# Low halves of the plain feed-forward, projection and gate weights: negated by ScalarE and completed by an adding transfer, instead of subtracted on VectorE

## The chip, the cores and the metric

The kernel runs on one core of one Trainium2 chip. The metric is the time of one execution on the device in microseconds (us); smaller is better. Several runs are taken and their median is compared. The profile is one further execution, recorded by the hardware. The core's engines are called here by the names that the profile uses: PE (TensorE, the matmuls), PEld (its weight loads), DVE (VectorE), ACT (ScalarE), POOL (GpSimd) and SP (SyncE, which issues transfers). Each engine works through its own queue in order, and waits on semaphores for the others.

## The reference

The kernel computes the trunk of a small encoder on 512 tokens of width 1024, in two layers. What matters here, cut from the reference:

```python
for i in range(DEPTH):                       # 2 layers
    h = h + 0.5 * swiglu(rmsnorm(h, ffn1_norm[i]), ffn1_w_gu[i], ffn1_w_down[i])
    hn = rmsnorm(h, mix_norm[i])
    h = h + (ssd_mixer(hn, ...) if i % 2 == 0 else neighbourhood_attention(hn, ...))
    h = h + 0.5 * swiglu(rmsnorm(h, ffn2_norm[i]), ffn2_w_gu[i], ffn2_w_down[i])
    gate = jax.nn.sigmoid(rmsnorm(h, ple_norm[i]) @ ple_w_gate[i])
    h = h + gate * rmsnorm(p[i] @ ple_w_proj[i], ple_post_norm[i])
```

`swiglu(x, w_gu, w_down)` splits `x @ w_gu` into a gate and an up half of 2816 columns each, and returns `(silu(gate) * up) @ w_down`. All of it is in 32-bit floating point.

## The kernel before

**Products in high and low halves.** A matmul of PE takes its operands in the type float32r, which holds fewer bits than float32. So the kernel splits each operand a into a high half, hi = a rounded to float32r, and a low half, lo = a - hi, and adds three products: hi by hi, hi by lo and lo by hi. In `gemm` these are lines 268, 271 and 272: line 268 multiplies the high half of the weights (`wh`) by the high half of the activations, line 271 the high half of the weights by the low half of the activations, and line 272 the low half of the weights (`wl`) by the high half of the activations. `block` does the same in lines 483, 484 and 485. An activation tile holds 512 tokens, so a matmul of `gemm` has 128 x 512 results, one of `block` 128 x 256.

**Units of weights.** Weights come in units of 128 partitions x 1024 numbers (512 KB), fewer for the down projections. A unit of 1024 feeds 24 matmuls: eight pieces of 128 rows, three products each. The generator `plan` writes down the order of all units of the program, ahead of the code that uses them. Its entries have a letter: "u" is a unit that is loaded and split; "g" loads a group of four, "s" forms sums and differences of them, "o" splits one of the results.

**Four steps of a unit.** `load_unit` (line 201) loads it by a transfer on SP into a raw buffer `wr`, of which there are four, up to three loads ahead. `split_raw` makes the halves: line 218, a copy on ACT from `wr` into `wh` that rounds, and line 220, a subtraction on DVE of `wh` from `wr` into `wl`. `wh` and `wl` have three buffers each. `unit` hands a unit to the matmuls; before it does, it prepares units until three are ready. So a unit is split as soon as the unit three places before it has left its buffers, that is, while PE works on the two units in between. The framework that builds the program turns all this into one queue for each engine, with the waits that the data and the buffers need, and it may queue instructions in another order than the text.

**The stages.** Each layer has four parts.

- A feed-forward part (`ffn`, four in the program). It begins with a *plain* stage: twelve units of `w_gu` (gate and up columns of the first six column blocks, `PLAIN`), one full `gemm` each, in `gate_up`. In all but the first part the first two of them run side by side, so that the factor of the norm can be formed meanwhile. During the plain stage DVE and ACT also form sums and differences of the activations (`sums`, lines 437 to 468) that the rest of the part needs. The rest is a *block* stage: eight pairs of column blocks by seven smaller products each, with the down projections between them (line 546 adds their results to `h`).
- In the first layer the state-space mixer (`ssd`), in the second the attention (`attention`).
- A second feed-forward part. Before its last eight down projections come the two units of `w_proj` (`ple_proj`), which feed eight products with two pieces each.
- A gate part (`ple`): eight units of `w_gate`, one `gemm` each. The activations of its norm are split by line 289 (ACT) and line 290 (DVE), each as soon as the last down projection of those rows has been added to `h` by line 546; their squares are summed by lines 310 (ACT) and 314 (POOL).

In the first feed-forward part of the program the first four plain units are loaded and split in halves by code of their own at the end of `trunk` (lines 1242 to 1247), not by `split_raw`.

**POOL's work around the change** is line 314 (sums of squares) and line 419 (the product of gate and up half), besides work in the mixer. No transfer is issued on POOL. `SCRATCH` sets aside 1024 bytes per partition for transfers that POOL issues.

Of the kernel before, what the change touches and what calls it, by code (L numbers as in the profile page):

```python
# [10 lines left out]
AF = mybir.ActivationFunctionType  # L11
ALU = mybir.AluOpType
# [36 lines left out]
def ffn_order():  # L49

    for f in range(PLAIN):
        yield "plain", f
    for c in range(1, len(CHUNKS)):
        a, b = CHUNKS[c]
        blocks = [(p, i) for p in range(a // 2, b // 2) for i in range(7)]
        d = 0
        for n, (p, i) in enumerate(blocks):
            yield "block", p, i  # L60
            while d < KD and (d + 0.5) * len(blocks) <= KD * (n + 1):
                yield "down", c - 1, d
                d += 1
    yield "between",
    for d in range(KD):
        yield "down", len(CHUNKS) - 1, d
# [3 lines left out]
def trunk(ctx, tc, A, out):  # L70
    nc = tc.nc
    v, s, g, te, sy = nc.vector, nc.scalar, nc.gpsimd, nc.tensor, nc.sync
# [13 lines left out]
    def nm(t):  # L86
        uid[0] += 1
        return f"{t}{uid[0]}"
# [54 lines left out]
    def plan():  # L143

        for i in range(stop):
            l, w = divmod(i, 4)
            if w in (0, 2):
                gu, gw, dn = [A[f"w_{x}{1 + w // 2}"][l] for x in ("gu", "gw", "dn")]  # L150

                def ahead(p, i_):
                    if i_ == 0:
                        yield "g", [gw[p - PLAIN // 2, x, y] for x, y in ((1, 0), (0, 0), (1, 1), (0, 1))]
                    yield "s", (p, i_)

                for what, *a in ffn_order():
                    if what == "plain":
                        for x in range(2):
                            yield "u", gu[a[0], x]  # L160
                            n = 2 * a[0] + x - (2 * PLAIN - 3)
                            if n >= 0:
                                yield from ahead(PLAIN // 2, n)
                    elif what == "block":
                        yield "o", a
                        if a[1] >= 4 and a[0] < NF // 2 - 1:
                            yield from ahead(a[0] + 1, a[1] - 4)
                    elif what == "down":
                        b = CHUNKS[a[0]]
                        yield "u", dn[a[1], :, b[0] * P:b[1] * P]  # L170
                    elif w == 2:
                        for n in range(2):
                            yield "u", A["w_proj"][l, n]
            elif w == 3:
                for n in range(KD):
                    yield "u", A["w_gate"][l, n]
            elif l % 2 == 0:
                for n in range(65):
                    yield "u", A["w_in"][n]
                for x in range(2):  # L180
                    for d in range(KD):
                        yield "u", A["w_out"][d, :, x * 1024:(x + 1) * 1024]
            else:
                for n in range(24):
                    yield "u", A["w_qkv"][n]
                for d in range(KD):
                    yield "u", A["w_ao"][d]

    todo = list(plan())

    loads = [x for what, a in todo if what in "gu"
             for x in (zip(a, ("wr", "wr", "md", "md")) if what == "g" else [(a, "wr")])]
    todo = iter(todo)
    raws, ready, splits, group, blocks = [], [], [], [], {}
    waiting = {"wr": 0, "md": 0}

    def load_unit():
        src, tag = loads.pop(0)
        raw = wp.tile([P, 1024], F32, name=nm("wr"), tag="wr", bufs=4) if tag == "wr" else wide()
        n = src.shape[-1]  # L200
        sy.dma_start(out=raw[:, :n], in_=src)
        raws.append((raw, n, tag))
        waiting[tag] += 1

    def take():
        if not raws:
            load_unit()
        raw, n, tag = raws.pop(0)
        waiting[tag] -= 1
        return raw, n  # L210

    def top_up():
        while loads and waiting[loads[0][1]] < {"wr": 3, "md": 2}[loads[0][1]]:
            load_unit()

    def split_raw(raw, n):
        hi = wp.tile([P, 1024], F32R, name=nm("wh"), tag="wh", bufs=3)
        splits.append(s.copy(out=hi[:, :n], in_=raw[:, :n]))  # L218
        lo = wp.tile([P, 1024], F32R, name=nm("wl"), tag="wl", bufs=3)
        v.tensor_sub(out=lo[:, :n], in0=raw[:, :n], in1=hi[:, :n])  # L220
        ready.append((hi, lo))

    def wide():
        return md().rearrange("p a b -> p (a b)")

    def prep_next():
        item = next(todo, None)
        if item is None:
            return False
        what, a = item  # L230
        if what == "u":
            split_raw(*take())
        elif what == "g":
            group[:] = [take()[0] for _ in range(4)]
        elif what == "s":
            p, i = a
            a21, a11, a22, a12 = group
            if i == 0:
                blocks[p] = {0: a11, 2: a21, 3: wide(), 4: a12, 6: a22}
                v.tensor_add(out=blocks[p][3], in0=a21, in1=a22)  # L240
            elif i == 1:
                blocks[p][1] = blocks[p][5] = wide()
                v.tensor_sub(out=blocks[p][1], in0=blocks[p][3], in1=a11)
            else:
                v.tensor_sub(out=a21, in0=a11, in1=a21)
        else:
            p, i = a
            b = blocks[p]
            split_raw(b[i], 1024)
            if i == 1:  # L250
                v.tensor_sub(out=b[5], in0=b[4], in1=b[5])
        top_up()
        return True

    def unit():
        while len(ready) < 3 and prep_next():
            pass
        return ready.pop(0)
# [969 lines left out]
    n = Norm(C_G1)  # L1228
# [36 lines left out]
    def first(pts, pairs):  # L1265
        done_ = [0] * 4
        here, cut_ = 0, [0] * 4
        for o in order:
            if isinstance(o, int):
                here = o + 1  # L1270
            else:
                cut_[o[0]] += 1
            for u in range(4):
                while done_[u] < min(here, 4 * cut_[u]):
                    k = done_[u]
                    gemm(pts[u], begun[u][2:], pairs[k:k + 1], first=k == 0, last=k == KD - 1, off=k)
                    done_[u] += 1
        while len(ready) < 3:
            prep_next()

        with tc.issue_after(splits[-1].ins):
            for k in range(KD):
                n.count(k, True)

    for i in range(stop):
        l, w = divmod(i, 4)
# [11 lines left out]
        n = m  # L1298
# [99 lines left out]
```

## Time and profile before

| what | value |
|---|---|
| runs | 2351.93, 2351.70 and 2353.02 us; median 2351.93 us |
| the profiled execution | 2352.96 us |
| its span, first to last instruction | 2351.2 us |
| mean clock granted to PE | 0.997 of full |
| transfers on SP's queue | 263.57 MB, 34.8% of the transfer engines' time |
| read from memory / written | 253.40 MB / 10.26 MB |

How to read the lines of the profile that follow. Times are us from the start of the span unless marked ns. A row of the timeline is: start, duration, engine, source line, operation, what it writes `<-` what it reads (tiles by name: `ps` is a matmul's result, `md` and `sc` are activations, `hs` is `h`, `t` a temporary), the shape, the count, and in brackets how long its engine had been idle before it and which instruction ended that. A row that groups instructions by line has the count and the shortest, median and longest duration in ns, then the starts of the first and the last of them. A row of a stretch of the span has the busy time of each engine in it, the clock granted to PE, and the share of time in which the 16 transfer engines were busy. Rows of transfers give the size of one and the median time from its issue to its landing. A matmul's duration overlaps with that of the next: at full speed 128 x 512 matmuls start about 0.23 us apart although each is shown as 0.39 us long.

Where the parts lie in the span, by the rows of the trace: the first feed-forward part up to about 370 us, its plain stage up to about 75; the state-space mixer up to about 923; the second feed-forward part from there, with its plain stage up to about 990 and its projection units at 1250; the first gate part from 1285 to 1339; the third feed-forward part with its plain stage from there; the attention from about 1660; the last feed-forward part from about 1935, its projection units at 2262, and the last gate part from 2296 to the end.

### The profile page before, as it was taken

To read this page: it belongs to the slowest core of one execution; us is meant where nothing else is said; L and a number is where in the kernel's file an instruction comes from. 1 tells how busy PE (TensorE), PEld (TensorE's weight loads), DVE (VectorE), ACT (ScalarE), POOL (GpSimd) and SP (SyncE) were. 2 spreads that over 40 slices of the span, in tenths; PEclk is the share of its full clock that TensorE was granted. 3 is DMA by queue.
4 is the path that set the end of the run, shared out by engine and by line. 5 is a ranking of instruction groups with operands and counts; after the bars stand their busy time and mean duration, and the time that the engine had idled before them with its cause. 6 is when DMAs were issued, how large, how long until landed. Compare 5 with 4: busy or idle time off the path is not lost.

```text
span 2351.2 us, 35169 instructions
## 1 busy us (share of the span) xinstructions
PE 2327.4 (99%) x13810; PEld 2026.6 (86%) x13810; DVE 1805.7 (77%) x2565; ACT 1111.8 (47%) x1819; POOL 353.7 (15%) x309
## 2 busy tenths in 40 slices
PE   9999999999999999999999999999999999999998
PEld 8899998888888888899997889999877888999987
DVE  7878868877777747978877897887778757777767
ACT  5433445755655653433345443334437744334353
POOL 1000001444445551100003110000100011000020
PEclk9999999999999999999999999999999999999999
DMA  5233324544444543323322332332433233333222
GB/s 191 84 101 104 108 72 131 172 138 138 143 136 142 162 162 107 115 84 104 108 86 84 103 115 85 104 108 77 145 121 130 103 100 100 111 108 99 81 81 81
DMA packets 99238, 265.95 MB, mean 113 GB/s; under 512 B 12016, under 2 KB 12912, under 8 KB 99072
## 3 DMA queue, kind: packets, MB, share of 16 engines
q1 hardware_dynamic: 98784, 263.57, 34.8%
q8 instruction: 108, 1.77, 0.3%
q14 instruction: 58, 0.48, 0.1%
q10 hardware_dynamic: 288, 0.14, 0.0%
HBM read 253.40 MB, written 10.26 MB: 112 GB/s over the span
## 4 chain that ended last, share of the span: by engine, by line
PE 90%; DVE 5%; ACT 1%; issue 1%; POOL 1%; DMA 1%; SPq 0%; POOLq 0%; ACTq 0%; DVEq 0%
PE ps L268 19%; PE ps L271 19%; PE ps L272 19%; PE ps L485 9%; PE ps L484 9%; PE ps L483 9%; PE ps L866 1%; DVE wl L220 1%; PE ps L844 1%; PE ps L887 1%; PE ps L800 1%; PE ps L786 1%; PE ps L1172 1%; DVE md L290 1%; DVE md L287 1%
## 5 line engine op out<-in xcount | busy, mean ns | idle before, releaser
L268 PE MATMUL ps<-md,wh 128*128 128x512 f32 x2128 | 838.4, 395 | 2.7 <-ACT md L286 2.1
L272 PE MATMUL ps<-md,wl 128*128 128x512 f32 x2128 | 830.7, 391 | 4.7 <-DVE wl L220 4.7
L271 PE MATMUL ps<-md,wh 128*128 128x512 f32 x2128 | 831.3, 391 | 0.7 <-DVE md L290 0.5
L218 ACT CAST wh<-wr 128x1024 fp32r<-128x1024 f32 (+2 forms) x401 | 358.1, 894 | 521.4 <-PE ps L271 199.9
L220 DVE TENSOR_TENSOR wl<-wr,wh 128x1024 fp32r<-128x1024 f32 (+2 forms) x401 | 429.0, 1070 | 114.1 <-ACT wh L218 85.3
L272 PEld LDWEIGHTS ps<-md,wl 128*128 128x128 f32 x2128 | 400.1, 188 | 90.7 <-DVE wl L220 6.7
L268 PEld LDWEIGHTS ps<-md,wh 128*128 128x128 f32 x2128 | 400.5, 188 | 84.4 <-issue 3.5
L271 PEld LDWEIGHTS ps<-md,wh 128*128 128x128 f32 x2128 | 400.9, 188 | 81.1 <-issue 3.3
L314 POOL TENSOR_TENSOR sq<-sq,sq 128x512 f32<-128x512 f32 x71 | 101.1, 1424 | 1444.8 <-ACT sq L310 1444.0
L218 ACT CAST wh<-md 128x1024 fp32r<-128x1024 f32 x160 | 167.7, 1048 | 297.8 <-PE ps L484 263.0
L483 PE MATMUL ps<-sc,wh 128*128 128x256 f32 x896 | 253.8, 283 | 4.2 <-ACT wh L218 4.2
L485 PE MATMUL ps<-sc,wl 128*128 128x256 f32 x896 | 254.3, 284 | 0.8 <-DVE wl L220 0.8
L484 PE MATMUL ps<-md,wh 128*128 128x256 f32 x896 | 254.1, 284 | 0.0
L485 PE MATMUL ps<-md,wl 128*128 128x256 f32 x896 | 254.1, 284 | 0.0
L484 PE MATMUL ps<-sc,wh 128*128 128x256 f32 x896 | 254.1, 284 | 0.0
L483 PE MATMUL ps<-md,wh 128*128 128x256 f32 x896 | 253.9, 283 | 0.0
L489 DVE TENSOR_TENSOR t<-ps,t 128x512 f32<-128x512 f32 x224 | 151.7, 689 | 129.8 <-PE ps L485 127.9
L220 DVE TENSOR_TENSOR wl<-md,wh 128x1024 fp32r<-128x1024 f32 x160 | 196.5, 1228 | 26.8 <-ACT wh L218 26.7
L483 PEld LDWEIGHTS ps<-sc,wh 128*128 128x128 f32 x896 | 172.1, 192 | 8.4 <-ACT wh L218 4.6
L484 PEld LDWEIGHTS ps<-sc,wh 128*128 128x128 f32 x896 | 172.2, 192 | 3.7
L484 PEld LDWEIGHTS ps<-md,wh 128*128 128x128 f32 x896 | 172.4, 192 | 1.2
L483 PEld LDWEIGHTS ps<-md,wh 128*128 128x128 f32 x896 | 172.4, 192 | 1.2
(207 smaller groups left out, 2859.8 us busy)
## 6 DMA issues: line engine op xcount, KB each, us to landing
wr<-in_w_in_dram SPq DMA_DIRECT2D x65, 512.0 KB, 3.5
wr<-in_w_gw_dram SPq DMA_DIRECT2D x64, 512.0 KB, 4.1
md<-in_w_gw_dram SPq DMA_DIRECT2D x64, 512.0 KB, 5.0
wr<-in_w_dn_dram SPq DMA_DIRECT2D x128, 256.0 KB, 2.7
wr<-in_w_gu_dram SPq DMA_DIRECT2D x44, 512.0 KB, 3.5
hs<-crow SPq DMA_DIRECT2D x64, 256.0 KB, 3.9
wr<-in_w_dn_dram SPq DMA_DIRECT2D x32, 384.0 KB, 3.1
wr<-in_w_qkv_dram SPq DMA_DIRECT2D x24, 512.0 KB, 3.7
```

What stands on the lines that cost most here:

```text
L218: splits.append(s.copy(out=hi[:, :n], in_=raw[:, :n]))
L220: v.tensor_sub(out=lo[:, :n], in0=raw[:, :n], in1=hi[:, :n])
L268: m = te.matmul(out=pt, lhsT=hi[:, sl], rhs=part(xp, 0, cols), start=first and k == 0, stop=False)
L271: te.matmul(out=pt, lhsT=hi[:, sl], rhs=part(xp, 1, cols), start=False, stop=False)
L272: te.matmul(out=pt, lhsT=lo[:, sl], rhs=part(xp, 0, cols), start=False, stop=last and k == n - 1)
L287: v.tensor_sub(out=dst[:, 1, :], in0=src, in1=dst[:, 0, :])
L290: v.scalar_tensor_tensor(out=dst[:, 1, :], in0=src, scalar=gain, in1=dst[:, 0, :], op0=ALU.mult, op1=ALU.subtract)
L314: (v if fast else g).tensor_add(out=self.acc, in0=self.acc, in1=q)
L483: te.matmul(out=o, lhsT=hi[:, sl], rhs=xh, start=j == 0 and kk == 0, stop=False)
L484: te.matmul(out=o, lhsT=hi[:, sl], rhs=xl, start=False, stop=False)
L485: te.matmul(out=o, lhsT=lo[:, sl], rhs=xh, start=False, stop=j == 1 and kk == 3)
L489: v.tensor_add(out=k[to], in0=pt, in1=k[other])
```

## The change

Units of the plain stages, of `w_proj` and of `w_gate` get a letter of their own in `plan`, "a". For them the low half is made without DVE. ACT reads the raw buffer a second time and writes its negative into the low half's buffer; that buffer has the type float32r, so what stands there is -hi. Then POOL issues a transfer that reads the same 512 KB of weights from memory once more and adds them to what stands in the buffer: the result is the weight minus hi, rounded to float32r as before. All other units keep the subtraction. `take` now hands on the source of the unit as well, so that the second transfer knows it.

```diff
                     if what == "plain":
                         for x in range(2):
-                            yield "u", gu[a[0], x]
+                            yield "a", gu[a[0], x]
...
                         for n in range(2):
-                            yield "u", A["w_proj"][l, n]
+                            yield "a", A["w_proj"][l, n]
             elif w == 3:
                 for n in range(KD):
-                    yield "u", A["w_gate"][l, n]
+                    yield "a", A["w_gate"][l, n]
...
-    def split_raw(raw, n):
+    def split_raw(raw, n, src=None):
         hi = wp.tile([P, 1024], F32R, name=nm("wh"), tag="wh", bufs=3)
         splits.append(s.copy(out=hi[:, :n], in_=raw[:, :n]))
         lo = wp.tile([P, 1024], F32R, name=nm("wl"), tag="wl", bufs=3)
-        v.tensor_sub(out=lo[:, :n], in0=raw[:, :n], in1=hi[:, :n])
+        if src is None:
+            v.tensor_sub(out=lo[:, :n], in0=raw[:, :n], in1=hi[:, :n])
+        else:
+            s.activation(out=lo[:, :n], in_=raw[:, :n], func=AF.Copy, scale=-1.0)
+            g.dma_start(out=lo[:, :n], in_=src, accum_op=ALU.add)
         ready.append((hi, lo))
...
-        if what == "u":
+        if what == "a":
             split_raw(*take())
+        elif what == "u":
+            split_raw(*take()[:2])
```

The entries of `raws` and the result of `take` get the source as a further member, and the list `loads` counts the letter "a" like "u". The first four plain units of the program stay as they were.

More of the change, by code (lines that the diff above doesn't have):

```diff
@@ L189, in trunk @@
     todo = list(plan())
-    loads = [x for what, a in todo if what in "gu"
+    loads = [x for what, a in todo if what in "agu"
              for x in (zip(a, ("wr", "wr", "md", "md")) if what == "g" else [(a, "wr")])]
@@ L201, in load_unit @@
         sy.dma_start(out=raw[:, :n], in_=src)
-        raws.append((raw, n, tag))
+        raws.append((raw, n, tag, src))
         waiting[tag] += 1
@@ L207, in take @@
             load_unit()
-        raw, n, tag = raws.pop(0)
+        raw, n, tag, src = raws.pop(0)
         waiting[tag] -= 1
-        return raw, n
+        return raw, n, src
     def top_up():
```

## The prediction

> **What bounds the kernel now.** I read the page's busy times and its chain first, then stretches of the span, then the waits inside the two stretches where the matmul engine (PE) is not full.
>
> ```profile
> span 2351.2 us, 35169 instructions
> PE 2327.4 (99%) x13810; PEld 2026.6 (86%) x13810; DVE 1805.7 (77%) x2565; ACT 1111.8 (47%) x1819; POOL 353.7 (15%) x309
> ...
> PE 90%; DVE 5%; ACT 1%; issue 1%; POOL 1%; DMA 1%; SPq 0%; POOLq 0%; ACTq 0%; DVEq 0%
> ```
>
> PE is busy for 2327.4 of 2351.2 us. The 23.8 us that are left hold the start and the tail too, so taking work off VectorE (DVE) can win only a few us, in places where PE visibly waits. Anything that makes PE wait costs its whole length.
>
> ```profile
> core 0: us, PE busy (x) PEld busy (x) DVE busy (x) ACT busy (x) POOL busy (x), PEclk, DMA share, GB/s
> 60.00:80.00 20.00, 15.81 (x71) 12.49 (x69) 19.86 (x33) 9.84 (x16) 1.55 (x1) 0.99 0.28 92
> 80.00:100.00 20.00, 19.18 (x107) 17.52 (x108) 16.79 (x20) 6.36 (x9) 2.07 (x1) 0.84 0.32 93
> 960.00:980.00 20.00, 20.00 (x90) 16.58 (x89) 19.09 (x30) 9.45 (x15) 1.64 (x1) 1.00 0.31 96
> 1280.00:1300.00 20.00, 17.85 (x74) 13.86 (x73) 18.52 (x31) 8.85 (x12) 4.52 (x3) 0.91 0.34 111
> 2290.00:2310.00 20.00, 16.68 (x73) 12.60 (x73) 18.70 (x24) 8.86 (x12) 5.32 (x4) 1.00 0.41 132
> ```
>
> The first two rows are the end of the plain stage of the first feed-forward part: DVE is full (19.86 of 20), PE loses 4.19 us, and in the next 20 us the granted clock is 0.84. The third row is the same stage of the second feed-forward part: DVE is nearly as full (19.09), yet PE has no gap; there DVE relief wins nothing. The last two rows are the starts of the two gate stages, with 2.15 and 3.32 us of PE idle beside a busy DVE.
>
> **The change, part by part.** It touches these units:
>
> ```profile
> wr<-in_w_gu_dram SPq DMA_DIRECT2D x44, 512.0 KB, 3.5
> ...
> wr<-in_w_gate_dram SPq DMA_DIRECT2D x16, 512.0 KB, 3.5
> ...
> wr<-in_w_proj_dram SPq DMA_DIRECT2D x4, 512.0 KB, 3.9
> ```
>
> That is 44 + 16 + 4 = 64 units (the four half-loaded ones at the start are formed elsewhere and stay). Each loses one DVE subtraction and gains one ScalarE (ACT) instruction and one GpSimd (POOL) transfer of 512 KB, 33.6 MB in all.
>
> ```profile
> L220 DVE TENSOR_TENSOR wl<-wr,wh x4: 1212/1216/1222, 51.1 to 65.9; 128x1024 fp32r<-128x1024 f32 x4
> ```
> ```profile
> L218 ACT CAST wh<-wr x2: 1040/1046/1052, 2293.7 to 2294.7; 128x1024 fp32r<-128x1024 f32 x2
> ```
>
> A subtraction is 1.22 us, so DVE gets 78 us lighter. The negation on ACT has the size of the cast, 1.05 us (two casts start 1.0 apart), so ACT gets about 67 us heavier, from 1111.8: it has room. Neither total is on PE's path; what counts is when a low half is ready.
>
> Let X be the time from the end of the negation to the landing of the added transfer. No row shows a POOL transfer or an added one. The nearest rows:
>
> ```profile
> wr<-in_w_dn_dram SPq DMA_DIRECT2D x128, 256.0 KB, 2.7
> ```
> ```profile
> L201 SPq DMA_DIRECT2D wr<-in_w_gu_dram x44: 327/328/388, 12.5 to 1978.2; - x44
> ```
>
> A plain load of 256 KB lands in 2.7 us and one of 512 KB in 3.5, 0.8 more per 256 KB. The added transfer must also fetch the 512 KB it adds to. If that counts like bytes loaded, it lands as 1 MB would, 5.1 us (an extrapolation). For the issue I add 0.7, about twice SP's 0.33. So X = 5.8. The low end is 3.5 (reading back is free); the high end is 7.0 (two loads in series), or 8.3 with one DVE instruction of about 1.2 us blocking on top. I take the middle because the step from 256 to 512 KB says bytes cost something.
>
> [...] No run here shows a POOL transfer yet.
>
> Now the places, each as "cast start + 2.0 (cast and negation) + X, against PE's first use".
>
> First feed-forward part (gain). DVE's four subtractions of the row above fall in the stretch that ends in PE's wait:
>
> ```profile
> 78.32 0.62 ACT L467 CAST md<-t 128x512 fp32r<-128x512 f32 x1 [2.53 <-DVE t L464]
> 78.85 1.04 ACT L218 CAST wh<-md 128x1024 fp32r<-128x1024 f32 x1
> ```
> ```profile
> 75.36 0.40 PE L271 MATMUL ps<-md,wh 128*128 128x512 f32 x1
> 79.94 0.58 PE L483 MATMUL ps<-sc,wh 128*128 128x256 f32 x1 [4.19 <-ACT wh L218]
> ...
> 81.55 0.58 PE L485 MATMUL ps<-sc,wl 128*128 128x256 f32 x1 [0.82 <-DVE wl L220]
> ```
> ```profile
> 86.41 0.42 PE L272 MATMUL ps<-md,wl 128*128 128x512 f32 x1
> ```
>
> PE waits 4.19 us for ACT, whose cast stands behind L467, which waits for DVE's backlog. Four subtractions less, 4 x 1.2 = 4.8 us, bring that forward by about the whole wait. What is late next is the low half behind the 0.82 wait, still DVE's. From 79.94 to 86.41 PE needs 6.47 us for the 24 matmuls of one block, 256 columns each; at half the 0.227 us of a 512-column one (worked out below) it would be 2.7, so 3.8 are lost, the 0.82 among them, and about 2.9 to the clock. Of the two gate stages, both with a wait of some 2 us, one lost clock (0.91) and the other didn't (1.00), so a short wait need not cost clock, and I count two thirds of the 2.9. Gain 4.2 + 1.9, about 6.0; bounds 3 (half the backlog moves) and 8.0 (all of it).
>
> Gate stages, two (about nothing). The first gate unit of the second one:
>
> ```profile
> 2296.39 0.39 PE L268 MATMUL ps<-md,wh 128*128 128x512 f32 x1
> 2296.62 0.39 PE L271 MATMUL ps<-md,wh 128*128 128x512 f32 x1
> 2299.06 0.50 PE L272 MATMUL ps<-md,wl 128*128 128x512 f32 x1 [2.06 <-DVE wl L220]
> ```
> ```profile
> L220 DVE TENSOR_TENSOR wl<-wr,wh x3: 1209/1214/1700, 2297.8 to 2304.3; 128x1024 fp32r<-128x1024 f32 x3
> ```
> ```profile
> L268 PE MATMUL ps<-md,wh x1: 387/387/387, 2306.2 to 2306.2; 128*128 128x512 f32 x1
> ```
> ```profile
> L268 PE MATMUL ps<-md,wh x18: 389/389/389, 2284.8 to 2296.4; 128*128 128x512 f32 x18
> ```
>
> Full speed is 11.56 us for 17 groups of three (last row), 0.68 a group, 0.227 a matmul, 5.44 a unit of 24. The unit begins at 2296.39 and its last group, held back by DVE's chain for the next norm, at 2306.21, so it ends at 2306.9. Afterwards DVE's chain is 3.9 us shorter (three subtractions), but the low half lands at 2293.7 + 2.0 + 5.8 = 2301.5 instead of before 2299.06. With 22 matmuls of 0.227 to go the unit ends at 2306.6. So one wait takes the place of another: no change at X = 6, a loss of 1 us for each us beyond, a gain below, up to 3.5. I take 0 for both.
>
> Projection units, two (a small loss). Cast and first use of the low half:
>
> ```profile
> L218 ACT CAST wh<-wr x1: 1047/1047/1047, 1244.0 to 1244.0; 128x1024 fp32r<-128x1024 f32 x1
> ```
> ```profile
> L272 PE MATMUL ps<-md,wl x1: 395/395/395, 1252.3 to 1252.3; 128*128 128x512 f32 x1
> ```
>
> 1244.0 + 2.0 + 5.8 = 1251.8, half a us before 1252.3. But two negations, 2.1 us, now stand on ACT ahead of the casts that PE's first matmul there waits for, and ACT, idle about half of the time, takes up perhaps 1.5 of it. Loss 0.6 each, 1.2 together, bounds 0 and 4.2 (both in full).
>
> Third-from-first plain unit of the other three feed-forward parts (nothing, with little to spare):
>
> ```profile
> L218 ACT CAST wh<-wr x2: 1037/1044/1050, 932.7 to 933.6; 128x1024 fp32r<-128x1024 f32 x2
> ```
> ```profile
> L272 PE MATMUL ps<-md,wl x1: 393/393/393, 941.1 to 941.1; 128*128 128x512 f32 x1
> ```
>
> 932.7 + 2.0 + 5.8 = 940.5 against 941.1: hidden up to X = 6.4, then 1 us per us, three times.
>
> All other plain and gate units are cast two units of PE ahead, 10.9 us, against 2.0 + 5.8: hidden up to X of about 8, counting a us of queueing. On POOL the transfer waits for ACT's negation; behind it stand only the gated product and the sums of squares, and POOL is idle 85% of the time. The raw buffer is no longer read by DVE, so loads on SP can start earlier; they are not waited for now. What the new queue costs at the start and end no row shows; outside the span lie 1.8 us now, so 0 to 1.8, I take 0.5.
>
> Sum: -6.0 + 0 + 1.2 + 0 + 0.5 = -4.3 us. The profiled execution took 2352.96 us (span 2351.2), 1.03 above the median of the three runs; 2352.96 - 4.3 - 1.03 = 2347.6, so about 2348 us as a median.
>
> **The rivals.** A difference of 0.2%, 4.7 us, is about what a measurement of this kernel can tell from no change.
>
> Late landing (slower). X is 7.6 or more, so the third plain unit, the first projection unit and the first gate unit make PE wait: beyond about 6.3 every us of X costs 7 us in those seven places. At X = 8.3: 2 x 2.4 + 2 x 2.0 + 3 x 1.9 = 14.5, so 2348 + 14.5 = 2362; with 3 instead of 6 us won in the first part, 2365. It is slower than before by 0.2% from X of about 7.6. A cause would be POOL held up by the busy DVE while it prepares transfers. For it: DVE is 93 to 99% busy exactly there, and the same bytes are handled twice. Against it: POOL is nearly idle and the transfer engines are 28 to 41% busy in those rows. Chance 0.25.
>
> [...]
>
> Early landing (faster still). X of 4.7 or less and the whole stall of the first part gone: -8.0, gates -1.2 each, projection and queue +0.6: 2352.96 - 1.03 - 9.8 = 2342. For it: 3.5 us for the plain load. Chance 0.18.
>
> Stall not moved. The backlog of DVE in the first part is refilled by its other work, or late low halves there replace it: the 6 us are not won and the result is 2354, about no change. This is also what comes out if the order in which the framework queues the instructions shifts against PE. Chance 0.12.
>
> **How the numbers follow.** My forecast, X between 4.7 and 7.6 and most of the stall gone, has a chance of 0.45 and its own range 2344 to 2355. Faster by over 0.2% (below 2347.2): the early landing 0.18 and a third of the forecast 0.16, together 0.34. Slower (above 2356.6): the late landing 0.24, and 0.04 from the forecast and the unmoved stall, together 0.28. Within: 0.38. The range goes from the early landing with a us to spare, 2341, to the late landing with the smaller gain, 2366.
>
> **What would show it.** Right: L220 has 64 instructions fewer; PE's wait of 4.19 us for ACT near 80 us is under 1.5 us; the 80 to 100 us stretch has a clock above 0.9; the POOL transfers land in 5 to 6.5 us; the first gate unit waits about 4.5 us for its low half instead of 2.1 and ends at the same distance from its start. Wrong: a wait of PE's low-half loads for transfers that repeats every 5.4 us through the plain stages (X above 8), or no shorter wait near 80 us.

## The result, and the profile after

The changed kernel takes 2382.9 us (median of 4 runs, 2378.31 to 2385.62) against 2351.9 for the kernel before beside it: ratio 1.0129, 95% interval 1.0111 to 1.0146. It is about 31 us slower; 2348 was forecast, and the late landing, the rival that came closest, had been put at 2362 to 2365. The profiled execution took 2382.52 us.

The head of the page and its chain of work:

```profile
span 2380.8 us, 35370 instructions
PE 2337.9 (98%) x13810; PEld 2032.5 (85%) x13810; DVE 1739.9 (73%) x2501; ACT 1170.4 (49%) x1883; POOL 409.6 (17%) x373
...
PE 65%; issue 24%; DMA 5%; DVE 3%; ACT 2%; POOL 1%; SPq 0%; POOLq 0%; DVEq 0%; ACTq 0%
```

In the chain, 21 of the 24% "issue" are two stretches of 254 us in which it follows POOL's queue back from a projection unit's transfer; PE was working meanwhile, so they are no cost.

DVE has 64 instructions fewer (2565 to 2501), ACT 64 more, and DVE is 66 us lighter: the change does what it says. The span is 29.6 us longer. PE's idle time went from 23.8 to 42.9 us, and its busy time from 2327.4 to 2337.9 for the same 13810 matmuls: 19.1 us more of waiting and 10.5 us more in the matmuls themselves.

What PE waited for (total, times, longest):

```profile
PE ps L278 <- DMA wl<-in_w_gate_dram: 14.9, 3, 6.7
PE ps L278 <- DMA wl<-in_w_gu_dram: 11.9, 7, 3.1
PE ps L278 <- DMA wl<-in_w_proj_dram: 4.7, 2, 2.7
```

Line 278 is the old line 272, the matmul with the low half of the weights. It waits 12 times, 31.5 us in all, for an adding transfer to land. These waits do not repeat every 5.4 us; they stand in a few places. Queues (packets, MB, share of the 16 transfer engines) and issues (count, size, median us to landing):

```profile
q1 hardware_dynamic: 98784, 263.57, 34.1%
q0 software_dynamic: 9216, 33.56, 8.0%
...
wr<-in_w_gu_dram SPq DMA_DIRECT2D x44, 512.0 KB, 5.2
wl<-in_w_gu_dram POOLq DMA_DIRECT2D x44, 512.0 KB, 7.9
...
wl<-in_w_gate_dram POOLq DMA_DIRECT2D x16, 512.0 KB, 7.4
wl<-in_w_proj_dram POOLq DMA_DIRECT2D x4, 512.0 KB, 6.8
```

The forecast had 5.8 us from the end of the negation to the landing. The transfer is issued 0.4 us after that end and lands 7.8 us later (median of the 64): 8.2. The plain loads beside it became slower too: 3.5 us before for `w_gu`, 5.2 now. From the two shares, one adding transfer of 512 KB takes 8.0% of 2380.8 / 64 = 3.0 us of all 16 engines; a plain 512 KB takes 34.1% of 2380.8 x 0.524 / 263.57 = 1.6.

Three stretches, the first and the second of which the prediction shows for the kernel before:

```profile
core 0: us, PE busy (x) PEld busy (x) DVE busy (x) ACT busy (x) POOL busy (x), PEclk, DMA share, GB/s
80.00:100.00 20.00, 18.44 (x120) 16.36 (x119) 15.76 (x19) 6.75 (x9) 3.26 (x1) 1.00 0.41 139
960.00:980.00 20.00, 19.73 (x87) 16.04 (x86) 17.14 (x27) 12.33 (x19) 5.91 (x6) 1.00 0.93 235
2320.00:2340.00 20.00, 13.26 (x50) 10.38 (x49) 10.90 (x24) 9.33 (x12) 6.31 (x6) 0.74 0.79 181
```

At 80 us the clock is back to 1.00 from 0.84 and the stall of 4.19 us is gone. In the plain stage near 960 us the transfer engines went from 0.31 to 0.93 busy. In the last gate part PE is busy 13.26 of 20 us, at a clock of 0.74.

The same matmul, by its number in PE's order, in both traces (after minus before, us, from PE's first matmul), read off where a part ends:

```
first feed-forward part   -3.0   (+2.2 up to 60 us, then -5.2 up to 90 us, past the old stall)
state-space mixer         -0.7
second feed-forward part  +5.5, its projection units +2.6
first gate part           +7.7
third feed-forward part   +5.2
attention                 -0.8
last feed-forward part    +6.0, its projection units +1.7
last gate part            +5.4
sum                      +29.6
```

### The profile page after: what moved, and what is told of

Same layout as the page of the kernel before. It is cut to its first block, busy times and chain, and to the rows that moved or that the text cites. A ratio compares the mean times of both kernels' runs of the same rounds, so it can differ in the third digit from the quotient of the medians.

```text
span 2380.8 us, 35370 instructions
## 1 busy us (share of the span) xinstructions
PE 2337.9 (98%) x13810; PEld 2032.5 (85%) x13810; DVE 1739.9 (73%) x2501; ACT 1170.4 (49%) x1883; POOL 409.6 (17%) x373
## 3 DMA queue, kind: packets, MB, share of 16 engines
q1 hardware_dynamic: 98784, 263.57, 34.1%
q8 instruction: 108, 1.77, 0.3%
## 4 chain that ended last, share of the span: by engine, by line
PE 65%; issue 24%; DMA 5%; DVE 3%; ACT 2%; POOL 1%; SPq 0%; POOLq 0%; DVEq 0%; ACTq 0%
PE ps L278 15%; PE ps L274 15%; PE ps L277 15%; PE ps L491 5%; PE ps L490 5%; PE ps L489 5%; DMA wl<-in_w_gu_dram 3%; PE ps L872 1%; PE ps L850 1%; PE ps L893 1%; DMA wl<-in_w_gate_dram 1%; PE ps L806 1%; PE ps L792 1%; PE ps L1178 1%; DMA wr<-in_w_gu_dram 1%
## 5 line engine op out<-in xcount | busy, mean ns | idle before, releaser
L278 PE MATMUL ps<-md,wl 128*128 128x512 f32 x2128 | 836.8, 393 | 32.3 <-DMA wl<-in_w_gate_dram 14.9
L221 DVE TENSOR_TENSOR wl<-wr,wh 128x1024 fp32r<-128x1024 f32 (+2 forms) x337 | 348.4, 1034 | 102.4 <-ACT wh L218 78.1
L221 DVE TENSOR_TENSOR wl<-md,wh 128x1024 fp32r<-128x1024 f32 x160 | 196.6, 1229 | 23.8 <-ACT wh L218 23.8
```

What stands on the lines that cost most here:

```text
L278: te.matmul(out=pt, lhsT=lo[:, sl], rhs=part(xp, 0, cols), start=False, stop=last and k == n - 1)
```

## The experiments

The theory: an added transfer lands in about the forecast 5.4 to 5.8 us alone, but shares the transfer engines with the plain loads; units cast shortly before their use then make PE wait. Rival A: the traffic itself slows everything. Rival B: 7.8 us is a fixed price, of the adding or of VectorE holding POOL up. Ratios are to the kernel before on the same chip; a count of us "by position" is the comparison just made.

### Only the first part

```diff
-                            yield "a", gu[a[0], x]
+                            yield "a" if i == 0 else "u", gu[a[0], x]
```

(and "u" for `w_proj` and `w_gate`.)

> Only the eight later plain units of the first feed-forward part are made by adding transfers; all other units keep the subtraction. Position by position the changed kernel was 5.0 us ahead of the kernel before at the end of that part. Theory (the added transfer lands late because it shares the transfer engines with plain loads, and only units cast shortly before their use make PE wait): the 5 us stay, 2347 us. Rival A (the transfers slow everything by their traffic alone, wherever they are): also about 2347, this run does not tell them apart. Rival C (the gain was an accident of the order and is given back at the next stage): 2352.

Measured 2349.2 us (11 runs), ratio 0.9988 (0.9979 to 0.9997). By position it is 2.9 us ahead at the end of the first part and stays ahead: 3.7 won from 60 us on, past the old stall, and 0.8 lost before, where three transfers are issued 1.9 us apart and land after 9 to 12 us. So the gain of this part is real. (The 5.0 of the expectation do not come out of the traces: the changed kernel is 3.0 ahead at the end of that part and 3.7 behind the mixer.)

### The tight units exempt

```diff
-                            yield "a", gu[a[0], x]
+                            yield "u" if i and a[0] < 2 else "a", gu[a[0], x]
...
-                    yield "a", A["w_gate"][l, n]
+                    yield "a" if n > 1 else "u", A["w_gate"][l, n]
```

(and "u" for `w_proj`.)

> 20 units get their subtraction back: the first four plain units of the three later feed-forward parts, the four projection units, the first two units of each gate part. 44 of 64 adding transfers stay. Theory (only units cast shortly before their use make PE wait): nearly all of the loss goes, 2347 to 2351 us, and PE waits for transfers less than 3 us in all against 31.5. Rival A (traffic alone): two thirds of the traffic stay, so about two thirds of the 36 us of losses less the 5 gained, 2369 us.

Measured 2358.1 us (8 runs), ratio 1.0024 (1.0014 to 1.0033): between the two expectations. PE's waits for transfers:

```profile
PE ps L278 <- DMA wl<-in_w_gu_dram: 5.1, 5, 1.4
...
PE ps L278 <- DMA wl<-in_w_gate_dram: 1.5, 1, 1.5
```

25 of the 31.5 us are gone with 20 of the 64 transfers, so the loss goes with the place, not with the traffic. But the list of places was too short: the five waits lie in the plain stages from their middle on. Their transfers are issued 6.9 to 9.2 us ahead of PE's need and land after 8.1 to 9.7 us, beside loads of the groups of four that the block stage needs.

### A spare target

```diff
+        v.tensor_sub(out=lo[:, :n], in0=raw[:, :n], in1=hi[:, :n])
+        if src is not None:
+            for c in (slice(0, 512), slice(512, 1024)):
+                g.dma_start(out=spare, in_=src[:, c], accum_op=ALU.add)
```

> Every subtraction is kept, no negation; beside it POOL issues the same adding transfers, in two halves of 256 KB, into a spare buffer that nobody reads. Same bytes, no reader. Theory (the loss is PE waiting for the low half): as the kernel before, 2352 us within 3. Rival A (traffic alone slows the plain loads and with them PE): most of the loss without the gain, 2375 or more. The landing of a 256 KB half: 3.5 to 5 us by the theory; close to 7 by rival B (a fixed price of an adding transfer, or VectorE holding POOL up while it prepares it).

Measured 2616.2 us (4 runs), ratio 1.1126 (1.1111 to 1.1141). It says nothing on rival A: there is one spare buffer, so each transfer stands at the head of POOL's queue until the one before has landed, and POOL's other work behind it is late. Nor do the transfers stand at the places of their units: all 128 are issued in the first 632 of 2614 us.

```profile
POOL spare L225 <- DMA spare<-in_w_gu_dram: 342.4, 86, 7.3
...
ACT sq L317 <- POOL sq L321: 205.1, 4, 195.8
```

One wait of ACT for POOL's sums is 195.8 us long. The landing of a 256 KB half is 4.1 us, as the theory had it.

### A copy in place of the addition

```diff
-            g.dma_start(out=lo[:, :n], in_=src, accum_op=ALU.add)
+            g.dma_start(out=lo[:, :n], in_=src)
```

> The changed kernel with plain transfers in place of the adding ones: they overwrite the negative, so what stands in the low halves is the whole weight and the output is another one. Theory (a 512 KB add takes about 3.1 us of all 16 transfer engines and shares them with loads): the copy takes about 1.6, lands in 4.5 to 5.5 us instead of 7.8, and the loss falls by two thirds or more, to 2350 to 2360 us. Rival B (POOL's issue, held up by VectorE, is what is late): landing stays at 7 to 8 us and the time at 2375 to 2385.

Measured 2350.3 us (10 runs), ratio 0.9991 (0.9981 to 1.0), just inside the theory's range. (The low halves hold whole weights here, so only the times of this run count.) Queue and issues:

```profile
q0 software_dynamic: 9216, 33.56, 4.1%
...
wl<-in_w_gu_dram POOLq DMA_DIRECT2D x44, 512.0 KB, 5.0
...
wl<-in_w_gate_dram POOLq DMA_DIRECT2D x16, 512.0 KB, 4.7
```

The same bytes from the same engine's queue, beside the same busy VectorE, take 4.1% of the transfer engines instead of 8.0 (1.5 us each instead of 3.0) and land after 4.8 instead of 7.8. So a POOL held up by VectorE is not what is late; the issuing instruction takes 0.54 us here instead of 0.87, which is a tenth of the 3 us. Adding doubles the transfer's time on the engines, and these 1.5 us become 3 at the landing.

### Adds that nobody reads

```diff
+        v.tensor_sub(out=lo[:, :n], in0=raw[:, :n], in1=hi[:, :n])
+        if src is not None:
+            g.dma_start(out=raw[:, :n], in_=src, accum_op=ALU.add)
```

> Every subtraction is kept and there is no negation; after it POOL issues the same adding transfer of 512 KB, now into the raw buffer that has just been read, so that nobody reads the result. Same bytes at nearly the same places, no reader; the next load of that buffer waits for it, with three others ahead. Theory (the loss is PE waiting for the low half): 2352 us within 4. Rival A (the traffic itself): most of the loss without the gain, 2375 or more.

Measured 2367.6 us (4 runs), ratio 1.0065 (1.005 to 1.008): neither. The raw buffers stay taken until the transfer has landed, and the loads of SP wait for that:

```profile
SPq L201 <- DMA wr<-in_w_gu_dram: 269.7, 45, 12.3
```

By position the loss (2.8, 3.7 and 4.2 us) comes where the plain stages of the later parts end, and PE waits there for subtractions. So what this run costs is late loads, an effect of its own; it cannot separate the theory from rival A.

### The weights taken from the raw buffer

```diff
-            g.dma_start(out=lo[:, :n], in_=src, accum_op=ALU.add)
+            g.dma_start(out=lo[:, :n], in_=raw[:, :n], accum_op=ALU.add)
```

> The changed kernel, but the added transfer takes the weights from the raw buffer instead of from memory. The result is the same. The raw buffer now stays taken until the transfer has landed, so the next load into it starts after the transfer and not beside it. Theory (the landing is 5.4 us alone and 7.8 us because plain loads run beside it): the landing falls to 5.5 to 6.5 us and the time to 2350 to 2362 us. Rival B (7.8 us is the price of an adding transfer whatever runs beside it): landing 7.5 or more, 2375 to 2390 us.

Measured 2359.8 us (10 runs), ratio 1.0024 (1.0014 to 1.0034), within the theory's range for the time.

```profile
PE ps L278 <- DMA wl<-wr: 14.9, 12, 5.1
...
q0 software_dynamic: 9216, 33.56, 7.5%
...
wl<-wr POOLq DMA_DIRECT2D x64, 512.0 KB, 5.3
```

The transfer still takes 7.5% of the engines, 2.8 us each, but lands after 5.3 us, a little below the 5.5 to 6.5 expected. The next load into the buffer now follows it, where in the changed kernel both were set free by the same negation and ran side by side. An addition is thus not bound to take 7.8; the waits are 14.9 us instead of 31.5. One reservation: source and timing change together here.

### The negation first

```diff
-        splits.append(s.copy(out=hi[:, :n], in_=raw[:, :n]))
         lo = wp.tile([P, 1024], F32R, name=nm("wl"), tag="wl", bufs=3)
+            s.activation(out=lo[:, :n], in_=raw[:, :n], func=AF.Copy, scale=-1.0)
+        splits.append(s.copy(out=hi[:, :n], in_=raw[:, :n]))
```

> The changed kernel with the two instructions of ScalarE for a unit in the other order: the negation first, the cast second. The transfer can start 1.05 us earlier and the high half is ready 1.05 us later. Theory (PE waits for the low half): each of the 12 waits for low halves (31.5 us together) is about 1 us shorter, with the half clock behind them about 15 us less, 2363 to 2372 us; a few waits for high halves of 0 to 1 us may come. Rival A (the traffic itself): no change, 2380 to 2385 us.

Measured 2381.7 us (4 runs), ratio 1.0132 (1.0114 to 1.015): no change, and the expectation missed. The edit did not do what it says. The framework still queues the cast ahead of the negation in 51 of the 64 units, probably because `wh` is read for the last time one matmul before `wl`. At the first gate unit, where the order did change, the transfer stood on POOL behind a sum of squares (line 321): it was issued 0.7 us earlier by position and landed at most 0.4 us earlier. The run tells nothing apart.

### Two halves

```diff
-            g.dma_start(out=lo[:, :n], in_=src, accum_op=ALU.add)
+            for c in (slice(0, 512), slice(512, 1024)):
+                g.dma_start(out=lo[:, c], in_=src[:, c], accum_op=ALU.add)
```

> The changed kernel with each adding transfer in two of 256 KB, columns 0 to 511 first. PE needs the second half of the columns 4 x 0.68 = 2.7 us after the first. Theory (the landing is bytes that share the transfer engines): the first half lands 2 to 3 us earlier than the whole did, the second at about the same time plus one issue of 0.87 us, and the waits lose about half of their 31.5 us: 2360 to 2372 us. Rival B (a fixed price of each adding transfer): the second half lands later by several us, POOL is held up, 2385 us or more.

Measured 2367.4 us (4 runs), ratio 1.0062 (1.0047 to 1.0077), as the theory had it.

```profile
PE ps L279 <- DMA wl<-in_w_gate_dram: 10.5, 3, 5.0
PE ps L279 <- DMA wl<-in_w_gu_dram: 4.6, 8, 1.3
PE ps L279 <- DMA wl<-in_w_proj_dram: 4.4, 4, 1.8
```

19.5 us of waiting instead of 31.5, with the same bytes, 64 issues of 0.87 us more on POOL, and more engine time (8.5%).

### One unit earlier

```diff
+    def negate():
+        raw, n, src = take()
+        lo = wp.tile([P, 1024], F32R, name=nm("wl"), tag="wl", bufs=4)
+        s.activation(out=lo[:, :n], in_=raw[:, :n], func=AF.Copy, scale=-1.0)
+        g.dma_start(out=lo[:, :n], in_=src, accum_op=ALU.add)
+        begun_lo.append((raw, n, lo))
...
+            ready.append((hi, lo))
+            if ahead_todo and ahead_todo[0][0] == "a":
+                negate()
```

> The changed kernel with the negation and the adding transfer of a unit issued one unit of PE earlier, when the unit before it is cast, wherever the next entry of the plan is such a unit too. The low halves get a fourth buffer, for which the activation tiles give up one of 24. All 64 transfers stay, with the same bytes. Theory (PE waits for low halves that land late, and for nothing else): the cover grows by 5.4 us, more than the 2.4 us by which the landing is late, so the waits fall from 31.5 us to 5 or less; where the plan has other entries between, in the second half of the plain stages, some stay. 2346 to 2356 us. Rival A (the traffic itself costs): most of the loss stays, 2370 or more.

> The kernel before with 23 instead of 24 activation tiles: what the missing tile costs by itself, which the run with the earlier transfers pays too. Both theories: 2352 to 2356 us.

With the transfers earlier: 2353.4 us (10 runs), ratio 1.0004 (0.9995 to 1.0013). The missing activation tile by itself: 2352.4 (10 runs), ratio 0.9998 (0.9988 to 1.0007), nothing. The waits of the earlier transfers, the issues, and two stretches in the plain stage of the second part:

```profile
PE ps L287 <- DMA wl<-in_w_gate_dram: 12.8, 2, 6.6
```
```profile
wl<-in_w_gu_dram POOLq DMA_DIRECT2D x44, 512.0 KB, 7.3
```
```profile
core 0: us, PE busy (x) PEld busy (x) DVE busy (x) ACT busy (x) POOL busy (x), PEclk, DMA share, GB/s
940.00:960.00 20.00, 20.00 (x90) 16.55 (x89) 15.44 (x26) 13.05 (x19) 7.07 (x6) 1.00 0.99 256
960.00:980.00 20.00, 20.00 (x90) 16.57 (x89) 17.26 (x26) 10.78 (x17) 4.99 (x4) 1.00 0.56 126
```

This is the run that decides against rival A. All 64 transfers are there, they still land late (7.3 us), the transfer engines are 0.99 busy, and PE is busy 20.00 of 20 us. In the plain stages and at the projection units no wait for a transfer is left. Only the first unit of each gate part waits, 6.6 us at most: ahead of it in the plan stands a down projection, so nothing is issued earlier there. The 5 us of remaining waits that I had expected were too few (12.8), and the place that I had named for them was wrong.

### The first part from the raw buffer, and the edits that helped joined

> Only the eight later plain units of the first feed-forward part are made by adding transfers, and these take the weights from the raw buffer. With all 64 made so, the kernel was 4.5 us ahead at the end of that part, against 2.9 us with the transfer from memory. Theory: 4.5 us stay, 2348 us. Rival (the difference between the two is noise of one profile): as with the transfer from memory, 2349 us; the interval may not tell these apart.

Measured 2348.1 us (11 runs), ratio 0.9982 (0.9973 to 0.999). By position 4.7 us ahead at the end of the first part, as expected, though the interval overlaps that of the transfer from memory. Nor is the difference between the two profiles the source's alone: in both, PE waits 1.34 us for ACT near 84 us, and only the transfer from memory has a stretch of 3.4 us at half clock behind that wait, which costs it 1.4 of the 1.8 us.

The last run joins what had helped: one unit earlier, from the raw buffer, and the subtraction kept for the gate units:

```diff
-                    yield "a", A["w_gate"][l, n]
+                    yield "u", A["w_gate"][l, n]
...
-        g.dma_start(out=lo[:, :n], in_=src, accum_op=ALU.add)
+        g.dma_start(out=lo[:, :n], in_=raw[:, :n], accum_op=ALU.add)
```

> The kernel with the transfers one unit earlier, with two edits: the gate units get their subtraction back, and the transfers take the weights from the raw buffer. With the earlier transfers PE's only waits for transfers were in the two gate parts, where the unit ahead of the first gate unit is a down projection, so that nothing is issued earlier there: 12.8 us in two waits. Theory: outside the gate parts the run with earlier transfers was 4.3 us ahead at 877 us, 1.5 and 1.3 more at the projection units and about 0.7 elsewhere; without the loss in the gate parts about 7 stay, 2345 us, 2343 to 2349. Rival A (the traffic itself): not under 2350.

Measured 2344.8 us (6 runs), ratio 0.9969 (0.9956 to 0.9981): faster than the kernel before by 0.3% and than the changed one by 38 us. No matmul waits for a transfer; the longest list of PE's waits is again that for subtractions, of which two, 2.05 us each, are those of the gate parts:

```profile
span 2342.5 us, 35274 instructions
...
PE 2323.8 (99%) x13810; PEld 2025.8 (86%) x13810; DVE 1764.7 (75%) x2517; ACT 1157.6 (49%) x1867; POOL 393.0 (17%) x357
```
```profile
PE ps L287 <- DVE wl L220: 4.7, 3, 2.1
```

By position the gains are 4.4 us in the first part, 1.5 at each pair of projection units and 0.7 each in the mixer and the attention: 9.0. Of the old stall a wait of 2.78 us for a subtraction is left.

## Why the prediction was wrong

**The stall of the first part: right.** The 4.19 us for ACT and the 0.82 behind it became one wait of 0.75 us, and no half clock followed:

```profile
77.94 0.39 PE L491 MATMUL ps<-sc,wl 128*128 128x256 f32 x1 [0.75 <-DVE wl L221]
```

By 85 us 6.6 us were gained there against the 6.0 forecast. Two terms were not in the sum: the 2.2 us lost before, to transfers that landed late among each other, and about 1.7 lost behind, where PE now waits for a cast of ACT, and shortly after for DVE, which the kernel before did not:

```profile
85.60 0.51 PE L274 MATMUL ps<-md,wh 128*128 128x512 f32 x1 [1.34 <-ACT md L292]
```

**X: the step that failed.** The prediction put "if that counts like bytes loaded, it lands as 1 MB would, 5.1 us" and added 0.7. As the price of a transfer by itself that was good. The last four transfers, for the last gate units, beside which no weights are loaded, land after 5.4 us; a stretch before, beside five loads, they take 7.8 (each row from its own window):

```profile
wl<-in_w_gate_dram POOLq DMA_DIRECT2D x4, 512.0 KB, 5.4
```
```profile
wr<-in_w_gate_dram SPq DMA_DIRECT2D x5, 512.0 KB, 4.1
wl<-in_w_gate_dram POOLq DMA_DIRECT2D x4, 512.0 KB, 7.8
```

5.4 and the 0.4 before the issue are 5.8. What failed is taking this for the price in the stream. The rival's X of 8.3 is what was measured (8.2), with another cause: no run shows the blocking VectorE instruction of 1.2 us that is in the 8.3, and the landing goes with the plain loads beside it, as the table below has it. The argument against a late landing, "the transfer engines are 28 to 41% busy in those rows", read the share of the kernel before and left out what the change adds to it. A unit of PE is 5.44 us long, and 3.0 us of all engines in each is 55% more: 0.31 + 0.55 = 0.86, and 0.93 was measured. Over the traces of the changed kernel, of the tight units exempt and of the earlier transfers, 58 transfers were issued with no other added one in flight (or one that landed within 0.1 us). By how long plain packets kept an engine, on the mean of the 16, in the 5.4 us after the issue:

```
plain packets    transfers   landing us, median (range)   VectorE busy of 5.4 us, median
under 1.0 us          8      5.5  (5.4 to 6.0)            4.1
1.0 to 1.5           12      6.2  (5.3 to 7.3)            4.3
1.5 us and more      38      8.0  (6.7 to 9.7)            3.7
```

The landing follows the plain packets. It does not follow VectorE, which is about equally busy in all rows: the cause that the prediction named for a late landing, POOL held up by the busy VectorE, does not show. The loads beside became slower as well: those of `w_gu` landed after 3.5 us before and after 5.2 now. How an engine shares its time between the two queues was not shown. How much of the stretch is due to the plain loads and how much to the preceding adding transfers, of which most units have one still in flight, was not separated; nor was the next adding transfer, which starts before the landing in 32 of the 38 of the last row and in 4 of the 8 of the first.

**Where it hit.** The rival had priced seven places at 1 us per us. At 8.3 that was 4.8 us for the gates, 4.0 for the projection units and 5.7 for the plain stages; measured were 13.1, 4.3 and 16.7. The projection units agree in sum only: PE's wait of 1.05 us there for a cast of ACT, which the forecast made longer, is gone (1.2 us won at each pair), and the low half, with half clock behind the first wait, costs 3.8 and 2.9. In the plain stages the third unit's transfer is issued 1.9 us ahead of the fourth's, among plain loads:

```profile
931.43 0.88 POOL L224 DMA_DIRECT2D wl<-in_w_gu_dram  x1 [9.38 <-ACT wl L223]
933.32 0.87 POOL L224 DMA_DIRECT2D wl<-in_w_gu_dram  x1 [1.01 <-ACT wl L223]
```
```profile
940.57 0.50 PE L278 MATMUL ps<-md,wl 128*128 128x512 f32 x1 [2.98 <-DMA wl<-in_w_gu_dram]
```

The first of them lands 9.1 us after its issue, at 940.5, and PE waits 3 us instead of none. "All other plain and gate units hidden" missed two more kinds of places: units in the second half of the plain stages, and the last gate unit of the first gate part (1.77 us).

**The clock: counted for the gain, forgotten for the loss.** The prediction saw that the old stall cost 2.9 us of clock and gave no clock to the waits that a late landing makes. In the last gate part the first low half comes 6.75 us late, and the matmul behind it has twice its usual 0.39 us:

```profile
2328.34 0.80 PE L278 MATMUL ps<-md,wl 128*128 128x512 f32 x1 [6.75 <-DMA wl<-in_w_gate_dram]
```

By the clock records of the trace, PE ran at half clock for 34.1 us between its first matmuls and the tail, before for 10.2, in stretches that are multiples of 3.41 us. In 7.3 of the 34.1 us and in 1.1 of the 10.2 PE was still waiting; the rest at half rate is 13.4 us lost against 4.6: 8.9 more, most of the 10.5 by which PE is busier. The clock fell behind five waits of 1.77 to 3.09 us too, all shorter than one such stretch. What a wait costs here is worked out in the last section.

**DVE's relief: right that it wins little elsewhere.** With 66 us less of DVE, the only other gains are 0.7 us in the mixer and 0.8 in the attention, where nothing was changed, and the 1.2 at each pair of projection units; the kernel before with 23 activation tiles shows 0.7 in the mixer too.

**The signs and the chances.** Three of the signs named for "right" held (64 instructions fewer on L220, no wait of 1.5 us or more near 80 us, a clock above 0.9 behind it); the landing of 5 to 6.5 us and the wait of 4.5 us at the first gate unit did not (7.8, and 6.4 and 6.75). Slower had been given 0.28, so the direction was not ruled out. The range ended at 2366 because the late landing had been given one value for X and no clock.

## What to carry to other kernels

A transfer that joins the critical path has two prices: alone, and with its own engine time and that of the loads beside it added to the share already there (here 5.4 and 7.8 us to the landing); work out the second before it is called hidden, and note what else the same instruction sets free. If a transfer lands late, issue it earlier rather than make it smaller: one unit ahead removed all waits in the plain stages with the engines 0.99 busy. Work moved off an engine that is not the bound helped here where PE was seen to wait behind that engine (of the 66 us taken off DVE, 5.2 us past the old stall, and at most 1.2 at any other place), so move it there alone.

## What the runs showed of the hardware that was not expected

- An adding transfer of 512 KB takes 3.0 us of all 16 transfer engines, a plain one on the same queue 1.5. Taken from the core's own buffer it is 2.8.
- Its issue on POOL takes 0.87 us (853 to 1125 ns) in the changed kernel, for 256 KB (spare target) and for 512 KB alike; a plain transfer's takes 0.54 (527 to 669 ns).
- Whether a wait costs clock is not a matter of its length alone. The waits of 1.77 us at the end of the first gate part and of 2.04 at the first projection units were followed by 3.4 us at half clock, those of 2.06 in the kernel before and of 2.68 at the second projection units by none; the 6.75 us cost 10.2 us at half clock. What fits is where the wait falls. In each of the 14 traces, between PE's first matmuls and the tail, the half clock begins and ends on a fixed grid of 3.41 us. Add up how long PE idles in one window of the grid at full clock: wherever it was 1.86 us or more, the next window ran at half clock; where it was under 1.55, it never did; between the two, both occur. (In the traces before and after alone: half clock behind 1.77 us and more, full behind 1.63 and less.) A window at half clock was followed by another one where PE idled 0.64 us or more in it, and by full clock where it was 0.47 or less. The 2.68 us lay in two windows, 1.63 and 1.05 us of them; the 2.04 lay in one.
